# A two-layer hybrid decoder trunk: products without use in the first stage, an interruptible output projection, and one small transfer moved in its queue

## The chip, the cores and the metric

The kernel runs on one NeuronCore of one Trainium2 chip. The metric is the device time of one execution in microseconds, the median of several runs. The core has five engines with a queue each. PE (TensorE) multiplies matrices; PEld is its loading of the stationary operand, which overlaps the products. DVE (VectorE), ACT (ScalarE) and POOL (GpSimd) work element by element. SP (SyncE) issues the transfers here. Each engine takes its instructions strictly in the order in which the program lists them; they wait for each other through semaphores.

## The reference

Two layers over 512 positions (T) of width 1024 (D), float32. Cut to what matters:

```
for l in range(2):
    h = rms_norm(x, norm_pre_mix[l])
    proj = h @ w_in[l]                    # attention q,k,v | delta q,k,v | gate | beta, decay
    mix = concat(dilated_attention(...), gated_delta_rule(...)) @ w_out[l]
    x = x + rms_norm(mix, norm_post_mix[l])
    h = rms_norm(x, norm_pre_ffn[l])
    u = causal_dwconv(h @ ffn_w_in[l], width 3) + bias
    f = (gelu(gate half of u) * up half of u) @ ffn_w_out[l]
    x = x + rms_norm(f, norm_post_ffn[l])
```

The beta and decay columns are 8 of the input projection's columns; everything in the delta rule hangs on them. `rms_norm` needs the sum of squares of a whole row of 1024, so no normed position can go on before both halves of its row are there.

## The kernel before, in words

**Tiling.** The 512 positions are four tiles of 128 positions, t = 0 to 3; x[t] is 128 positions by 1024. A projection wants the position on the free axis, so a normed tile xs is turned on PE (four 128x128 transposes into one PSUM bank for each half s of the row, s = 0, 1) and then split into a rounded part `hh` (ACT copies it out of PSUM as fp32r) and the rest `hl` (DVE subtracts). Weights are treated alike: the staged `st` gives `wh` (ACT) and `wl` (DVE or POOL). Each product is then three: rounded by rounded, and rounded by rest twice (`three`).

**Two projection helpers.** `chan_proj` gives channels by positions, a block of 128 channels at a time; its first four blocks (`early`) are done first for positions 0 to 255 alone (matmuls with 256 columns), so that they can begin when tiles 0 and 1 are turned; between them the turns of tiles 2 and 3 are issued (`turns`). `tok_proj` gives positions by channels, 128 by 512, with four PSUM banks, one for each t. The weights come in `npc` pieces of two 128-row parts; a call of `piece(pc, t)` is six matmuls of 512 columns. The last `tail` pieces are done tile by tile, and after the last of tile t comes `evac(t, ...)`.

**Output projection.** `out_proj` calls `tok_proj` twice, for columns 0 to 511 (`first`) and 512 to 1023 (`second`). All four pieces of the second half are tail pieces, so PE does tile 0 (four pieces, 24 matmuls), then tile 1, 2 and 3. `second` for a tile squares and sums on ACT (`junk<-pm`), takes the root on POOL (`pr`), adds into x[t] on DVE, and calls `after(t)`, which is `pre_norm`: sum of squares of x[t] on ACT (`junk<-x`), root on POOL (`nr`), the normed xs on DVE. `pre_norm` returns `turn`, the function that issues the eight transposes, hh and hl of that tile. The list `turns` holds these functions. Before the change `out_proj` pops one turn after tile 2 is finished and one after tile 3; the other two go to the up-projection's `chan_proj` (`w_f1`, the profile's `in_w_f`), whose first product needs tiles 0 and 1 turned.

**First stage** (layer 0 only). x[0] comes in two transfers and x[1] in one; then the weight `row` of the norm is spread over the partitions by two products of a row of ones (`pn`), copied to `nw`, and tiles 0 and 1 are normed, turned and split. `ident` is the identity matrix of the transposes. The first projection is `chan_proj` over four key blocks (`w_dn`, `late_low`: block 0 does its three kinds of product in three passes). Beside it runs `decay`, which loads the small weights `stb` (32 KB) of the 8 beta and decay columns, splits them (`wba`) and multiplies them with all four tiles.

**Order of the work.** A scheduler writes every engine's list ahead of time from priorities (`prio(pe, other)`, lower goes first, the first number for PE, the second for all others) and from its own estimate of when things are ready. The transfer queue of SP is ordered by the second number: 2.2 for x[2] and x[3], 2.5 for the tables, L + 3 (3 in layer 0, 103 in layer 1) for the decay part. A wait at the head of a list holds up all that stands behind it.

Of the kernel before, what the change touches and what calls it, by code (L numbers as in the profile page):

```python
# [9 lines left out]
F32 = mybir.dt.float32  # L10
# [24 lines left out]
class Engines:  # L35
# [8 lines left out]
    @contextmanager  # L44
    def prio(self, pe, other=None):
        saved = self.levels
        self.levels = (pe, pe if other is None else other)
        yield
        self.levels = saved
# [41 lines left out]
def run(gen):  # L91
    for _ in gen:
        pass
# [3 lines left out]
def hybrid_trunk(ctx: ExitStack, tc: tile.TileContext, a, out):  # L97
# [67 lines left out]
    def residual(t, src, parts=1):  # L165
        v = quad("x")
        n = D // parts
        for s in range(parts):
            nc.sync.dma_start(v.rearrange("p s n -> p (s n)")[:, s * n:s * n + n], src[:, s * n:s * n + n])
        return v  # L170
# [76 lines left out]
    def act_h(k, t):  # L247
        return hh[:, k, t * P:(t + 1) * P], hl[:, k, t * P:(t + 1) * P]

    def tok_proj(load, npc, get_l, tail, evac):  # L250


        ps = [pm.tile([P, T], F32, name="pm") for _ in range(NT)]
        w = {}

        def piece(pc, t):
            for kk in range(2):
                k = pc * 2 + kk
                wh, wl = w[pc][kk * len(w[pc]) // 2]
                k_ = kk % wh.shape[1]  # L260
                three(ps[t], *get_l(k, t), wh[:, k_, :], wl[:, k_, :], k == 0, k == npc * 2 - 1)

        for pc in range(npc - tail):
            w[pc] = load(pc)
            for t in range(NT):
                piece(pc, t)
            yield
        for pc in range(npc - tail, npc):
            w[pc] = load(pc)
        for t in range(NT):  # L270
            for pc in range(npc - tail, npc):
                piece(pc, t)
            evac(t, ps[t])
            yield

    def out_proj(load, npc, get_l, pnw, after, l0, l1, ln, keep_tile):

        keep, turns = {}, []

        def first(t, ps):  # L280
            with prio(ln):
                ss = sp.tile([P, 2], F32, name="pss", bufs=4)
                o = keep_tile(t)
                nc.scalar.activation(o, ps, AF.Copy)
                square_sum(o, ss[:, 0:1])
                nc.vector.tensor_tensor(o, o, pnw[0], op=OP.mult)
                keep[t] = (o, ss)

        def second(t, ps):
            with prio(ln):  # L290
                o, ss = keep[t]
                square_sum(ps, ss[:, 1:2], tag="junk2")
                r = rstd(ss, "p")
                tmp = ev("ptmp")
                nc.vector.tensor_tensor(tmp, ps, pnw[1], op=OP.mult)
                for s, src in ((1, tmp), (0, o)):
                    nc.vector.scalar_tensor_tensor(x[t][:, s, :], src, r, x[t][:, s, :], op0=OP.mult, op1=OP.add)
                turns.append(after(t))

        with prio(*l0):  # L300
            run(tok_proj(lambda pc: load(0, pc), npc, get_l, 2, first))
        with prio(*l1):
            steps = tok_proj(lambda pc: load(1, pc), npc, get_l, 4, second)
            for i, _ in enumerate(steps):
                if i - (npc - 4) >= 2 and turns[0]:
                    turns.pop(0)()
        return turns if turns[0] else []

    def chan_proj(w_src, nblk, early, evac, turns=(), eng=lambda b: None, late_low=False):

# [44 lines left out]
    for l in range(NL):  # L355
# [2 lines left out]

        if l == 0:
            with prio(0):  # L360
                x[0] = residual(0, a["x"][0, 0:P, :], 2)
                row = pair("row", (1, D))
                nc.sync.dma_start(row, a["norm_pre_mix"][0:1, :])
                x[1] = residual(1, a["x"][0, P:2 * P, :])
                nc.sync.dma_start(ident, a["ident"])
                pn, nw = [], []
                for s in range(2):
                    pn.append(ps4("pn", (P, T)))
                    nc.tensor.matmul(pn[s], ones[0:1, :], row[:, s * T:(s + 1) * T], start=True, stop=True)
            with prio(2.2):  # L370
                for t in range(2, NT):
                    x[t] = residual(t, a["x"][0, t * P:(t + 1) * P, :])
            with prio(4, 0):
                turns = [pre_norm(0, pn, 2)]
                turns[0]()
                for s in range(2):
                    nw.append(am("nw"))
                    nc.scalar.activation(nw[s], pn[s], AF.Copy)
                pre_norm(1, nw)()
            with prio(4, 2.1):  # L380
                turns = [pre_norm(t, nw) for t in range(2, NT)]

# [23 lines left out]

        def decay():
            stb = wp.tile([P, KC, 8], F32, name="stb", bufs=1)
            nc.sync.dma_start(stb, a["w_ba"][l])
            wba = wp.tile([P, KC, 16], F32R, name="wba", bufs=1)  # L410
            split(wba[:, :, 0:8], wba[:, :, 8:16], stb)
            pba = ps4(shape=(P, T))
            for k in range(KC):
                nc.tensor.matmul(pba[:16], wba[:, k, :], hh[:, k, :], start=k == 0, stop=False)
                nc.tensor.matmul(pba[:16], wba[:, k, :], hl[:, k, :], start=False, stop=k == KC - 1)
            bas = big("bas")
            nc.scalar.activation(bas[:16], pba[:16], AF.Copy)
            pb2 = ps4(shape=(P, NT, 8))
            for t in range(NT):
                nc.tensor.matmul(pb2[:, t, :], bas[:16, t * P:(t + 1) * P], fold, start=True, stop=True)  # L420
            xa, xb = s16("xa"), s16("xb")
            nc.scalar.activation(v3(xb), pb2[:, :, 0:4], AF.Exp, scale=-1.0)
            nc.vector.tensor_tensor(v3(xa), pb2[:, :, 4:8], dtb[:, None, l * H:(l + 1) * H].to_broadcast([P, NT, H]),
                                    op=OP.add)
            nc.vector.tensor_scalar(xb, xb, 1.0, None, op0=OP.add)
            nc.vector.reciprocal(bet, xb)
            yield
            na, e2, u, d1, cz, rd, lnu, sf = (s16(n) for n in ("na", "e2", "u", "d1", "cz", "rd", "lnu", "sf"))
            nc.vector.scalar_tensor_tensor(na, xa, -1.0, xa, op0=OP.mult, op1=OP.min)
            nc.scalar.activation(e2, na, AF.Exp)  # L430
            nc.vector.tensor_scalar(u, e2, 1.0, None, op0=OP.add)
            nc.scalar.activation(lnu, u, AF.Ln)
            nc.vector.tensor_scalar(d1, u, -1.0, None, op0=OP.add)
            nc.vector.tensor_scalar(cz, d1, 0.0, None, op0=OP.is_equal)
            nc.vector.tensor_tensor(d1, d1, cz, op=OP.add)
            nc.vector.reciprocal(rd, d1)
            nc.vector.tensor_tensor(sf, lnu, rd, op=OP.mult)
            nc.vector.tensor_tensor(sf, sf, cz, op=OP.add)
            nc.vector.tensor_tensor(sf, sf, e2, op=OP.mult)
            nc.vector.scalar_tensor_tensor(sf, xa, 0.0, sf, op0=OP.max, op1=OP.add)  # L440
            ea = sp.tile([P, H], F32, name="ea", bufs=1)
            nc.scalar.activation(ea, alog[:, l * H:(l + 1) * H], AF.Exp)
            nc.vector.scalar_tensor_tensor(v3(gr), v3(sf), -1.0, ea[:, None, :].to_broadcast([P, NT, H]),
                                           op0=OP.mult, op1=OP.mult)
            pg = ps4(shape=(P, 32))
            nc.tensor.matmul(pg[:, :16], tri, gr, start=True, stop=True)
            nc.tensor.matmul(pg[:, 16:], ones, gr, start=True, stop=True)
            nc.vector.tensor_scalar(ng, pg[:, :16], -1.0, None, op0=OP.mult)
            nc.scalar.activation(eg, pg[:, :16], AF.Exp)
            nc.vector.tensor_scalar(neg, eg, -1.0, None, op0=OP.mult)  # L450
            nc.scalar.activation(egl, pg[:, 16:], AF.Exp)

            pgt = ps4(shape=(P, P))
            nc.tensor.matmul(pgt[:16], gr, tri, start=True, stop=True)
            gt = sp.tile([16, P], F32, name="gt", bufs=1)
            nc.vector.tensor_copy(gt, pgt[:16])
            nc.sync.dma_start(dG, gt)
            for t in range(NT):
                Gs.append(big("G", shape=(P, H, P)))
                nc.sync.dma_start(Gs[t].rearrange("p h i -> p (h i)"), bcast(dG, H * P, t * H * P))  # L460
            nc.vector.tensor_tensor(bd, pg[:, 16:], ng, op=OP.add)
            nc.scalar.activation(bd, bd, AF.Exp)
            yield
# [656 lines left out]
```

## Time and profile before

| what | value |
| --- | --- |
| median of 3 runs | 1332.97 us (1331.96 to 1333.19) |
| the profiled execution's own time | 1331.07 us |
| its span | 1329.3 us |
| PE busy in the span | 1297.5 us (98%), 6892 matmuls |
| PE waiting before the first product | 4.2 us |
| PE waiting for ACT's hh, whole span | 4.9 us, 4 times, longest 2.2 us |
| PE waiting for DVE's xs, whole span | 4.9 us, 7 times, longest 1.1 us |
| PE waiting for DVE's wba | 0.7 us, once |

The profiled execution took 1.9 us less than the median of the runs, and its span is 1.8 us shorter than its own time. In the profile's rows a start in us from the span's start is followed by a duration, the engine, the source line (here always that of a helper, L54), the operation, out<-in by the names of the program, the shape, and how many instructions were merged (x8). In brackets stands the idle time of the engine ahead of the row and what ended it. The window rows give, for a stretch, its length, then busy time and number of instructions of PE, PEld, DVE, ACT and POOL, then the granted clock of TensorE (PEclk), the busy share of the DMA engines, and GB/s. Ends of matmuls are modelled, so the distance from start to start tells more than a duration.

### The profile page before, as it was taken

The page shows a single profiled execution, that of the slowest core. Times are in us where ns is not written, and L with a number is a line of the kernel's source. Part 1 is how long each engine was busy: PE and PEld are TensorE (multiplying, and loading weights), DVE is VectorE, ACT ScalarE, POOL GpSimd, SP SyncE. Part 2 cuts the span into 40 slices and gives each one's busy share as a digit, 9 for nine tenths or more (in the row PEclk, how much of TensorE's full clock was granted, in tenths as well). Part 3 has the DMA queues.
Part 4 walks back from the last instruction along what each step waited for, and adds up shares of the span by engine and source line. Part 5 has one row for each costly group of instructions (what it writes and reads, how often), then busy time and mean ns, then how long its engine had stood idle before and what let it go on. Part 6 is the DMA issues. An engine that isn't in the chain of part 4 may idle for free.

```text
span 1329.3 us, 19287 instructions
## 1 busy us (share of the span) xinstructions
PE 1297.5 (98%) x6892; PEld 1082.3 (81%) x6892; DVE 1005.4 (76%) x1938; ACT 728.0 (55%) x1466; POOL 179.4 (13%) x222
## 2 busy tenths in 40 slices
PE   8999999998999999999999999999999999999997
PEld 7787888878888888888778877888888888888876
DVE  6766888967676788798778568989667677888885
ACT  5635976754433344467547369676543334444673
POOL 0019400201000000030011292002010000001201
PEclk9999999999999999999999999999999999999999
DMA  7233211344466566366652422104436565653664
GB/s 241 84 103 96 72 53 37 111 143 135 139 229 212 174 222 218 106 187 180 215 170 77 122 81 76 52 17 135 134 113 208 188 221 203 226 173 116 194 189 159
DMA packets 75425, 193.14 MB, mean 145 GB/s; under 512 B 13345, under 2 KB 13889, under 8 KB 75330
## 3 DMA queue, kind: packets, MB, share of 16 engines
q1 hardware_dynamic: 74882, 190.87, 44.9%
q0 software_dynamic: 448, 1.05, 0.3%
q8 instruction: 54, 0.88, 0.3%
q14 instruction: 41, 0.34, 0.1%
HBM read 161.99 MB, written 29.90 MB: 144 GB/s over the span
## 4 chain that ended last, share of the span: by engine, by line
PE 72%; DVE 6%; ACT 3%; issue 2%; POOL 2%; DMA 1%; POOLq 0%; DVEq 0%; ACTq 0%; SPq 0%
PE pm L54 62%; PE pw L54 10%; DVE wl L54 2%; ACT junk L54 1%; DVE xs L54 1%; DVE x L54 1%; POOL nr L54 1%; DMA st<-in_w_f 1%; ACT wh L54 1%; DVE xf L54 1%; POOL pr L54 1%; DVE hl L54 0%; POOL qs L54 0%; ACT sc L54 0%; DMA G<-dG 0%
## 5 line engine op out<-in xcount | busy, mean ns | idle before, releaser
L54 DVE TENSOR_TENSOR wl<-st,wh 128x1024 fp32r<-128x1024 f32 (+1 forms) x250 | 281.9, 1133 | 167.1 <-ACT wh L54 166.0
L54 ACT ACTIVATE wh<-st 128x1024 fp32r<-128x1024 f32 (+1 forms) x254 | 245.6, 971 | 245.5 <-PE pm L54 225.3
L54 PE MATMUL pm<-hh,wh 128*128 128x512 f32 (+1 forms) x1024 | 372.2, 366 | 4.9 <-ACT hh L54 4.9
L54 PE MATMUL pm<-hh,wl 128*128 128x512 f32 (+1 forms) x1024 | 373.7, 366 | 1.1 <-DVE wl L54 1.1
L54 PE MATMUL pm<-hl,wh 128*128 128x512 f32 (+1 forms) x1024 | 373.5, 366 | 0.0
L54 PEld LDWEIGHTS pm<-hh,wh 128*128 128x128 f32 x1024 | 194.1, 191 | 35.8 <-ACT hh L54 6.2
L54 PEld LDWEIGHTS pm<-hh,wl 128*128 128x128 f32 x1024 | 194.7, 191 | 30.7 <-DVE wl L54 1.3
L54 PEld LDWEIGHTS pm<-hl,wh 128*128 128x128 f32 x1024 | 194.8, 191 | 28.9
L54 PE MATMUL pm<-wh,xf 128*128 128x512 f32 x528 | 164.5, 390 | 0.0
L54 PE MATMUL pm<-wh,hh 128*128 128x512 f32 x384 | 153.3, 401 | 0.0
L54 PE MATMUL pm<-wl,hh 128*128 128x512 f32 x384 | 152.3, 398 | 0.0
L54 PE MATMUL pm<-wh,hl 128*128 128x512 f32 x384 | 151.2, 396 | 0.0
L54 DVE SCALAR_TENSOR_TENSOR fgu<-pm,fw,fgu 128x511 f32<-128x511 f32 (+1 forms) x176 | 131.2, 746 | 21.9 <-ACT fgu L54 19.9
L54 PEld LDWEIGHTS pm<-wh,xf 128*128 128x128 f32 x528 | 99.1, 188 | 21.3 <-ACT e L54 0.6
L54 PE MATMUL pm<-wl,xf 128*128 128x512 f32 x264 | 103.5, 392 | 0.5 <-DVE wl L54 0.5
L54 POOL TENSOR_TENSOR g<-g 128x256 f32<-128x256 f32 x22 | 25.3, 1168 | 493.2 <-DVE xf L54 493.2
L54 PEld LDWEIGHTS pm<-wh,hh 128*128 128x128 f32 x384 | 71.9, 188 | 14.9 <-DVE zs L54 0.6
L54 PEld LDWEIGHTS pm<-wh,hl 128*128 128x128 f32 x384 | 72.4, 189 | 14.0
L54 PEld LDWEIGHTS pm<-wl,hh 128*128 128x128 f32 x384 | 72.4, 189 | 13.6 <-DVE wl L54 0.8
L54 ACT ACTIVATE fgu<-fgu 128x512 f32<-128x512 f32 x44 | 27.8, 632 | 90.4 <-DVE fgu L54 90.4
L54 ACT ACTIVATE fgu<-pm,fb,fw 128x512 f32<-128x512 f32 x88 | 66.9, 760 | 18.6 <-PE pm L54 18.6
L54 ACT ACTIVATE xf<-g 128x256 fp32r<-128x256 f32 x154 | 60.2, 410 | 29.2 <-PE pm L54 22.5
(228 smaller groups left out, 1796.3 us busy)
## 6 DMA issues: line engine op xcount, KB each, us to landing
st<-in_w_f SPq DMA_DIRECT2D x118, 512.0 KB, 3.7
ws<-in_w_f SPq DMA_DIRECT2D x88, 256.0 KB, 4.7
T<-ws SPq DMA_DIRECT2D x66, 256.0 KB, 2.3
st<-in_w_at SPq DMA_DIRECT2D x32, 512.0 KB, 4.0
st<-T SPq DMA_DIRECT2D x30, 512.0 KB, 4.0
st<-in_w_dn SPq DMA_DIRECT2D x24, 512.0 KB, 4.0
st<-in_w_out SPq DMA_DIRECT2D x16, 512.0 KB, 3.7
U<-ws SPq DMA_DIRECT2D x22, 256.0 KB, 2.2
```

What stands on the lines that cost most here:

```text
L54: r = f(*args, **kwargs)
```

## The change

Three things are changed.

**First stage.** PE gets seven products without use, 128 by 128 by 128 in f32, into a PSUM bank of their own (`pwarm`, one of the four `pm` banks): four of `ones` with itself at the very start, one with x[0] behind the two `pn` products, two with nw[0]. The transfer of `row` goes ahead of x[0]. x[1] comes in two transfers, and its squares are summed in two halves.

**Output projection.** `tok_proj` gets an optional function that is called after each tail piece. `out_proj` uses it to pop the turn of tile 0 after the third of the four pieces of tile 2, and that of tile 1 after the third piece of tile 3.

**Small weights.** The transfer `stb` gets its own priority (L + 2.3 in SP's queue): behind x[2] and x[3], ahead of the tables.

```
-    def tok_proj(load, npc, get_l, tail, evac):
+    def tok_proj(load, npc, get_l, tail, evac, between=None):
...
             for pc in range(npc - tail, npc):
                 piece(pc, t)
+                if between:
+                    between(t, pc - npc + tail)
             evac(t, ps[t])
...
         with prio(*l1):
-            steps = tok_proj(lambda pc: load(1, pc), npc, get_l, 4, second)
-            for i, _ in enumerate(steps):
-                if i - (npc - 4) >= 2 and turns[0]:
+            def between(t, i):
+                if (t, i) in ((2,2),(3,2)):
                     turns.pop(0)()
-        return turns if turns[0] else []
+
+            run(tok_proj(lambda pc: load(1, pc), npc, get_l, 4, second, between))
+        return turns
...
             with prio(0):
-                x[0] = residual(0, a["x"][0, 0:P, :], 2)
+                pwarm = pm.tile([P, T], F32, name="pm")
+                def warm(n, moving):
+                    for _ in range(n):
+                        nc.tensor.matmul(pwarm[:, :P], ones, moving[:, :P], start=True, stop=True)
+                warm(4, ones)
                 row = pair("row", (1, D))
                 nc.sync.dma_start(row, a["norm_pre_mix"][0:1, :])
-                x[1] = residual(1, a["x"][0, P:2 * P, :])
+                x[0] = residual(0, a["x"][0, 0:P, :], 2)
+                x[1] = residual(1, a["x"][0, P:2 * P, :], 2)
...
+                warm(1, x[0][:, 0, :])
...
+                warm(2, nw[0])
-                pre_norm(1, nw)()
+                pre_norm(1, nw, 2)()
...
         def decay():
             stb = wp.tile([P, KC, 8], F32, name="stb", bufs=1)
-            nc.sync.dma_start(stb, a["w_ba"][l])
+            with prio(L + 1, L + 2.3):
+                nc.sync.dma_start(stb, a["w_ba"][l])
```

The scheduler then writes other lists at three stretches: the first stage with what follows from it in layer 0, and the end of the output projection in each of the two layers. The down-projection and everything else keep their order.

**Place 1: the start of PE's list.** Before (pn is the spread norm weight, pw a bank of transposes, wh_218 and wh_222 the two halves of key block 0):

```order
L54 MATMUL pn<-row,ones 128x512 x2
L54 MATMUL pw<-ident,xs 128x128 x12
L54 MATMUL pm<-hh,wh_218 128x256 x4
L54 MATMUL pw<-ident,xs 128x128 x4
L54 MATMUL pm<-hh,wh_222 128x256 x4
```

Now (wh_229 and wh_233 are block 0, wh_278 is block 1):

```order
L54 MATMUL pm<-ones 128x128 x4
L54 MATMUL pn<-row,ones 128x512 x2
L54 MATMUL pm<-x,ones 128x128
L54 MATMUL pw<-ident,xs 128x128 x4
L54 MATMUL pm<-nw,ones 128x128
L54 MATMUL pw<-ident,xs 128x128 x4
L54 MATMUL pm<-nw,ones 128x128
L54 MATMUL pw<-ident,xs 128x128 x4
L54 MATMUL pm<-hh,wh_229 128x256 x4
L54 MATMUL pw<-ident,xs 128x128 x4
L54 MATMUL pm<-hh,wh_278 128x256
L54 MATMUL pm<-hl,wh_278 128x256
```

The products without use stand ahead of `pn`, behind it, and between the transposes of tiles 0 and 1. The 16 products of `wba`, which stood some 90 matmuls behind the transposes of tile 3, now follow them directly.

**Place 2: PE's list at the end of the output projection, layer 0.** Before (the wh_33xx are the output projection's weights, wh_3550, wh_3599 and wh_3648 blocks 0 to 2 of the up-projection):

```order
L54 MATMUL pm<-wh_3328,hh 128x512
L54 MATMUL pm<-wl_3329,hh 128x512
L54 MATMUL pm<-wh_3328,hl 128x512
L54 MATMUL pw<-ident,xs 128x128 x8
L54 MATMUL pm<-hh,wh_3550 128x256
L54 MATMUL pm<-hh,wh_3599 128x256
L54 MATMUL pm<-hh,wh_3648 128x256
L54 MATMUL pw<-ident,xs 128x128 x4
L54 MATMUL pm<-hl,wh_3550 128x256
```

Now:

```order
L54 MATMUL pw<-ident,xs 128x128 x8
L54 MATMUL pm<-wh_3335,hh 128x512
L54 MATMUL pm<-wl_3336,hh 128x512
L54 MATMUL pm<-wh_3335,hl 128x512
L54 MATMUL pm<-wh_3339,hh 128x512
L54 MATMUL pm<-wl_3340,hh 128x512
L54 MATMUL pm<-wh_3339,hl 128x512
L54 MATMUL pm<-hh,wh_3561 128x256
L54 MATMUL pm<-hh,wh_3610 128x256
L54 MATMUL pm<-hh,wh_3659 128x256
```

The eight transposes of tile 1 now have six matmuls of tile 3 behind them (those of tile 0 likewise six of tile 2). The first four transposes of tile 2, which stood ahead of `hl,wh_3550`, now stand 23 matmuls later together with the other four.

**Place 3: ACT's list at the same place.** Before (`junk<-x` is the sum of squares of the new x[t], `junk<-pm` that of the second half of the projection's tile, hh the rounded copy of a turned half tile; the first two rows are for tiles 2 and 3, the hh row is tile 1):

```order
L54 ACTIVATE junk,ss<-x 128x1024
L54 ACTIVATE junk,pss<-pm 128x512
L54 ACTIVATE hh<-pw 128x4x128 x2
L54 ACTIVATE wh_3687<-st 128x512
L54 ACTIVATE hh<-pw 128x4x128
L54 ACTIVATE wh<-st 128x1024 x2
L54 ACTIVATE hh<-pw 128x4x128
```

Now (the first hh row is tile 1, the second tile 2):

```order
L54 ACTIVATE hh<-pw 128x4x128 x2
L54 ACTIVATE junk,ss<-x 128x1024
L54 ACTIVATE junk,pss<-pm 128x512
L54 ACTIVATE wh_3698<-st 128x512
L54 ACTIVATE wh<-st 128x1024 x2
L54 ACTIVATE hh<-pw 128x4x128 x2
```

The two hh of tile 1 no longer stand behind the two sums. On DVE the two hl of tile 1, which stood behind the root `nv`, a weight split and the first half of xs of tile 2, now stand ahead of these three; the second half of xs of tile 1 stands behind the two hl of tile 0 instead of ahead of them.

## The prediction

> **What bounds the kernel now.** I read the page first, then PE's waits, then PE's timeline at its longest waits, with the windows' clock beside it.
>
> ```profile
> span 1329.3 us, 19287 instructions
> PE 1297.5 (98%) x6892; PEld 1082.3 (81%) x6892; DVE 1005.4 (76%) x1938; ACT 728.0 (55%) x1466; POOL 179.4 (13%) x222
> PE pm L54 <- ACT hh L54: 4.9, 4, 2.2
> PE pw L54 <- DVE xs L54: 4.9, 7, 1.1
> PE pn L54 <- DMA row<-in_norm_pre_mix: 4.2, 1, 4.2
> ```
>
> PE is the bound: it is busy 98% of the span, and no other engine over 76%. So a microsecond that PE doesn't wait, or doesn't work at half rate, is one off the end, if nothing later waits instead. The change cannot shorten PE's useful work; it can only touch waits and the clock. PE's waits for hh and xs sit where it hands over between stages. The first stage:
>
> ```profile
> 4.23 3.75 PE L54 MATMUL pn<-row,ones 1*128 1x512 f32 x4 [4.23 <-DMA row<-in_norm_pre_mix]
> 7.91 2.98 PE L54 MATMUL pw<-ident,xs 128*128 128x128 f32 x12
> 11.58 1.22 PE L54 MATMUL pm<-hh,wh 128*128 128x256 f32 x4 [0.69 <-ACT hh L54]
> 14.34 1.22 PE L54 MATMUL pm<-hh,wh 128*128 128x256 f32 x4 [0.69 <-ACT hh L54]
> 17.06 1.74 PE L54 MATMUL pm<-hl,wh 128*128 128x256 f32 x8
> 18.64 0.28 PE L54 MATMUL pm<-hh,wh 128*128 128x256 f32 x1
> 18.76 0.28 PE L54 MATMUL pm<-hl,wh 128*128 128x256 f32 x1
> 36.51 0.40 PE L54 MATMUL pw<-hh,wba 128*16 128x512 f32 x1 [0.74 <-DVE wba L54]
> ```
>
> Look at the spacing: eight matmuls of 256 columns take 1.74 us at 17.06, 0.217 each; from 18.64 on the same shape comes every 0.12. PE runs at half rate until about 18.5. The hand-over in the output projection, layer 0:
>
> ```profile
> 304.37 1.03 PE L54 MATMUL pw<-ident,xs 128*128 128x128 f32 x8
> 310.70 1.04 PE L54 MATMUL pw<-ident,xs 128*128 128x128 f32 x8
> 313.93 0.62 PE L54 MATMUL pm<-hh,wh 128*128 128x256 f32 x3 [2.19 <-ACT hh L54]
> 315.32 1.00 PE L54 MATMUL pw<-ident,xs 128*128 128x128 f32 x4 [0.76 <-DVE xs L54]
> 315.97 0.56 PE L54 MATMUL pm<-hl,wh 128*128 128x256 f32 x1
> 325.16 0.63 PE L54 MATMUL pw<-ident,xs 128*128 128x128 f32 x4 [0.54 <-DVE xs L54]
> 315.40:318.80 3.40, 3.40 (x17) 3.40 (x18) 3.34 (x7) 2.45 (x3) 0.55 (x1) 0.50 0.34 136
> 319.00:321.00 2.00, 2.00 (x20) 2.00 (x19) 0.78 (x2) 0.30 (x1) 0.00 (x0) 1.00 0.00 0
> ```
>
> PE has finished the projection and the turn of tile 1 by about 311.7, then stands still until 313.93 and again until 315.32. Right behind that the granted clock is 0.50 for 3.4 us: 17 matmuls where 20 come in 2.0 us at full clock. So the standstill is paid twice: 2.19 + 0.76 + 0.54 = 3.49 us of waits, and half of 3.4, 1.7 us, of slow work. In layer 1 the same:
>
> ```profile
> 969.47 0.62 PE L54 MATMUL pm<-hh,wh 128*128 128x256 f32 x3 [1.35 <-ACT hh L54]
> 970.86 1.09 PE L54 MATMUL pw<-ident,xs 128*128 128x128 f32 x4 [0.76 <-DVE xs L54]
> 980.66 0.63 PE L54 MATMUL pw<-ident,xs 128*128 128x128 f32 x4 [0.55 <-DVE xs L54]
> 970.00:975.00 5.00, 4.24 (x24) 4.18 (x24) 4.93 (x9) 2.91 (x4) 0.55 (x1) 0.66 0.43 156
> ```
>
> 1.35 + 0.76 + 0.55 = 2.66 us of waits; 0.34 of 5 us of clock lost is 1.7 us again.
>
> **The output projection's edit.** Who holds hh up? ACT and DVE, layer 0:
>
> ```profile
> 308.98 1.58 ACT L54 ACTIVATE wh<-st 128x1024 fp32r<-128x1024 f32 x2 [0.95 <-DMA st<-in_w_f]
> 311.67 1.06 ACT L54 ACTIVATE junk<-x 128x1024 bf16<-128x1024 f32 x1 [1.11 <-DVE x L54]
> 313.30 1.07 ACT L54 ACTIVATE hh<-pw 128x512 fp32r<-128x512 f32 x2
> 306.81 1.42 DVE L54 SCALAR_TENSOR_TENSOR xs<-x,nr,norm_pre_ffn 128x512 f32<-128x512 f32 x2 [0.67 <-POOL nr L54]
> 308.14 1.28 DVE L54 TENSOR_TENSOR hl<-pw,hh 128x512 fp32r<-128x512 f32 x2
> 311.49 1.82 DVE L54 TENSOR_TENSOR wl<-st,wh 128x512 fp32r<-128x512 f32 x2
> 315.09 1.28 DVE L54 TENSOR_TENSOR hl<-pw,hh 128x512 fp32r<-128x512 f32 x2
> ```
>
> ACT is free from 310.56, but the turn of tile 1 ends at 311.5, and by its list two sums come first, one of which waits for x. Now the turn stands six matmuls earlier: from 304.37 to 310.70 lie one turn (0.8) and 24 matmuls, so 0.23 each, 1.4 for six. Tile 0's turn starts at 304.37 - 1.4 = 303.0, tile 1's at 309.3. hh of tile 1 then runs at 310.56, behind wh, to 311.6. DVE, in its new order: xs first half to 307.5, hl of tile 0 to 308.8, xs second half to 309.5 (0.2 later than its place on PE; the first four transposes cover it), then the chain of tile 2 as before but 0.25 later, the wl pair to 313.4, hl of tile 1 at 313.4 instead of 315.09, its first half done at 314.1. PE: last six matmuls end at 311.5, the three `hh,wh` at 311.9, then a wait until 314.1 for hl, some 2.0 us. No transposes interrupt there now; those of tile 2 come 23 matmuls later, 2.8 us, at about 316.9, when their xs (two of 0.7 behind hl) is just done. What is late next is tile 3, the wait at 325.16. Its sum on ACT stands behind the second hh of tile 2, whose transposes now come with the first four, some 2 us earlier; so its xs is there at about 323.2. PE at full clock is there at about 322, so it waits about 1.0 where it waited 0.54. Waits left: 3.0 against 3.49, gain 0.5; and the half rate of 1.7 goes, if a standstill of 2.0 doesn't cost the clock. Layer 1: its first wait was 0.84 shorter than layer 0's, so it is about 1.2 now, and the last 1.0: 2.2 against 2.66, gain 0.46, and 1.7. I take 2.2 + 2.2 = **4.4 us**. If the clock still falls, PE reaches tile 3 too late to wait, and only 3.49 - 2.0 and 2.66 - 1.2, 3.0 together, is gained. Upper bound, the tile 3 wait hidden too: 6.4. From there to 660 PE's only wait is this one, so it keeps what it has:
>
> ```profile
> 620.35 0.50 PE L54 MATMUL pm<-wl,xf 128*128 128x512 f32 x1 [0.26 <-DVE wl L54]
> ```
>
> **The first stage's edit.**
>
> ```profile
> 0.75 0.86 SPq L54 DMA_DIRECT2D x<-in_x  x2
> 1.66 0.33 SPq L54 DMA_DIRECT2D row<-in_norm_pre_mix  x1
> 3.38 0.63 ACT L54 ACTIVATE junk<-x 128x512 bf16<-128x512 f32 x1 [1.36 <-DMA x<-in_x]
> 6.86 1.06 ACT L54 ACTIVATE junk<-x 128x1024 bf16<-128x1024 f32 x1 [2.00 <-DMA x<-in_x]
> 16.69 0.75 DVE L54 SCALAR_TENSOR_TENSOR xs<-x,nr,nw 128x512 f32<-128x512 f32 x1 [0.52 <-POOL nr L54]
> 8.00:10.00 2.00, 2.00 (x9) 1.67 (x10) 1.89 (x4) 1.95 (x5) 0.55 (x1) 1.00 1.02 420
> ```
>
> Cost of the products: a `pn` product of 512 columns is two instructions of about 0.85 (four from 4.23 to 7.9 with the drain), so one of 128 columns is a quarter, 0.43, and seven are 3.0 us. Four (1.7) lie in the 4.23 us in which PE waits for `row`; one lies behind `pn`, where PE waits for ident and xs; two (0.9) stand between transposes, ahead of the 0.69 wait for hh that covers most of them. Cost 0 to 0.5. `row` leaves 0.9 earlier and x[0] 0.35 later; x[0] then is the later one, gain 0 to 0.4. The extra transfer of x[1] takes SP about 0.4, hidden because the DMA engines are full (share 1.02, 420 GB/s) and the bytes stay in the same order. Data side: -0.3 to +0.4, taken as +0.2.
>
> The clock is the larger part. 24 matmuls of 256 columns and four transposes between 11.58 and 18.64 run at half rate: 24 x 0.097 + 0.45 = 2.8 us, if PE were the bound there. It isn't throughout: at full rate PE comes to tile 2's transposes at about 16.2 (14.34, less 1.0 for faster transposes and matmuls ahead of it, and 24 matmuls at 0.12), while their xs, paced by ACT and DVE, started at 16.69 and moves little. Bounds 0 and 2.8; I take 1.3, nearer the middle since half is lost to that wait.
>
> The Trainium skill (TensorE: Matmul & The Clock Gate, Part 1: The HAM clock gate) says that the array starts at half clock and is released after a free-running window of about 3.4 us of sustained work, and halved after an idle one; the 3.4 us of 0.50 above agree in length. By that rule PE, occupied by the products and `pn` from the start, would be released before the first transposes, and with the upper bound of 2.8 the time would be 1325.1.
>
> **stb's transfer.** The wait of 0.74 at 36.51 goes, since the split of `stb` now comes ten microseconds earlier; the 16 products now stand right behind tile 3's turn and may wait there for its hl instead. Between 0 and 0.74: 0.5. Tables pushed behind `st` (dmask, tri) are used after 36 us only.
>
> **Sum.** 4.4 + 0.2 + 1.3 + 0.5 = 6.4 us; span 1322.9. The profiled execution took 1331.07, 1.8 over its span and 1.9 under the median of the runs; I take the difference off that median: 1332.97 - 6.4 = **1326.6 us**.
>
> **Rivals.**
>
> *The clock falls again in the hand-over.* For it: 2.0 of 3.4 us still idle in layer 0. Against it: at least 1.4 us of work in any such stretch, where before under 1 us was left. Sum 3.0 + 2.0 = 5.0: 1328.0.
>
> *The early release doesn't happen, or is lost before block 0.* For it: `pn` kept PE occupied from 4.23 to 7.9 and twelve transposes to 10.9, yet the rate rose only at 18.5, after 4 us of dense matmuls. So the filler may count for little and transposes not at all. Sum without the 1.3: 5.1, so 1327.9. The Trainium skill states a rule for this (TensorE: Matmul & The Clock Gate, Part 4: PE-mode transpose): transposes don't count as busy work for the clock; the row at 7.91 agrees with it.
>
> *The turns move but hl doesn't.* hl of tile 1 stays behind tile 2's chain because ACT's hh is late (the split at 308.98 waits for its transfer) and lands where it was. Then only the first stage's 2.0 remains: 1331.0, no change. For it: that wait is a DMA's. Against: ACT has a whole microsecond free before 311.67.
>
> *Slower: PE blocks on a turn that isn't ready.* Once a turn stands inside a tile's matmuls, PE can't go round it. Tile 0's xs is ready 0.4 before its new place, tile 1's 0.2 after it. Were DVE late by D there, PE would stop for about D twice in each layer, 4D; it eats the gain from D = 1.6, and at 2.4 the time is 1332.97 - 6.4 + 9.6 = 1336.2. Against: DVE's chain there is the unchanged one, and D that large is not seen in either layer.
>
> **How the numbers follow.** Forecast 0.46, clock falls again 0.18, no early release 0.18, hl not earlier 0.11, slower 0.05, other 0.02. 0.2% is 2.7 us, about what a measurement of this kernel tells from no change; faster means under 1330.3, which holds for the first three: 0.82. Same 0.12, slower 0.06. Range: best bounds 6.4 + 0.4 + 2.8 + 0.7 = 10.3 down to 1322.7, unlikely together; the worst of the faster cases, both clock rivals at once, 1329.3, and most of the third: 1323.2 to 1330.8.
>
> **What would show it.** PE's spacing of 256-column matmuls at 0.12 before 14 us; the wait of 0.74 gone; the transposes of tiles 0 and 1 about 1.4 us earlier relative to the projection; one wait of 1 to 2 us on hl in the hand-over, no 0.50 in the windows behind it; a wait of about 1 us for tile 3's xs. Half clock behind the hand-over, or a wait on xs inside the output projection, would prove me wrong.

## The result, and the profile after

| | median | range, runs |
| --- | --- | --- |
| before | 1332.91 us | 1331.96 to 1333.19, 4 |
| changed | 1324.86 us | 1321.87 to 1326.42, 4 |

The ratio is 0.9934, with a 95% interval of 0.992 to 0.9948: 8.0 us by the medians, 8.8 by the ratio. The profiled execution of the changed kernel took 1325.45 us.

The head of the page of the changed kernel, and PE's part of its waits (total, times, longest):

```profile
span 1323.7 us, 19323 instructions
PE 1295.8 (98%) x6906; PEld 1080.4 (82%) x6906; DVE 1006.7 (76%) x1938; ACT 729.1 (55%) x1468; POOL 178.8 (14%) x222
```

```profile
PE pm L54 <- DVE hl L54: 2.2, 2, 1.1
PE pm L54 <- ACT hh L54: 1.0, 2, 0.7
PE pw L54 <- DVE xs L54: 5.0, 7, 1.6
```

PE's busy time is 1.7 us less with 14 more instructions: work was not removed, less of it ran at half rate. The wait for hh fell from 4.9 to 1.0, and a wait for hl of 2.2 in two places is new. PE's timeline of the changed kernel at the hand-over of the output projection, layer 0 and then layer 1, and below it the windows there:

```profile
309.26 1.03 PE L54 MATMUL pw<-ident,xs 128*128 128x128 f32 x8
313.08 0.39 PE L54 MATMUL pm<-hl,wh 128*128 128x256 f32 x1 [1.05 <-DVE hl L54]
322.67 0.63 PE L54 MATMUL pw<-ident,xs 128*128 128x128 f32 x4 [0.92 <-DVE xs L54]
966.47 0.39 PE L54 MATMUL pm<-hl,wh 128*128 128x256 f32 x1 [1.15 <-DVE hl L54]
976.01 0.63 PE L54 MATMUL pw<-ident,xs 128*128 128x128 f32 x4 [0.86 <-DVE xs L54]
```

```profile
313.00:315.00 2.00, 1.92 (x16) 1.93 (x17) 1.56 (x5) 0.12 (x1) 0.93 (x1) 1.00 0.75 277
315.00:317.00 2.00, 2.00 (x20) 2.00 (x19) 1.94 (x5) 1.12 (x2) 0.55 (x1) 1.00 0.48 188
968.00:970.00 2.00, 2.00 (x20) 2.00 (x19) 1.89 (x4) 1.06 (x1) 0.40 (x2) 1.00 0.60 244
```

Two waits remain in each layer, 1.97 and 2.01 us together where there were 3.49 and 2.66, and the clock stays at 1.00: 20 matmuls in 2.0 us where 17 had taken 3.4. Counted in matmuls, PE gains 3.2 us on the kernel before across layer 0's hand-over and 2.3 across layer 1's. The timeline of the changed kernel's first stage, PE's rows and the one of ACT that comes into them late:

```profile
1.06 2.07 PE L54 MATMUL pm<-ones 128*128 128x128 f32 x8 [1.06 <-DVE pexp L54]
3.07 3.78 PE L54 MATMUL pn<-row,ones 1*128 1x512 f32 x4
8.04 1.09 PE L54 MATMUL pw<-ident,xs 128*128 128x128 f32 x4 [0.46 <-DMA ident<-in_ident]
12.61 0.74 PE L54 MATMUL pm<-hh,wh 128*128 128x256 f32 x4 [0.69 <-ACT hh L54]
16.02 1.12 PE L54 MATMUL pm<-hl,wh 128*128 128x256 f32 x8
29.93 0.40 PE L54 MATMUL pw<-hh,wba 128*16 128x512 f32 x1 [0.71 <-ACT hh L54]
31.31 0.40 PE L54 MATMUL pw<-hl,wba 128*16 128x512 f32 x1 [0.50 <-DVE hl L54]
28.34 1.06 ACT L54 ACTIVATE wh<-st 128x1024 fp32r<-128x1024 f32 x1 [2.46 <-DMA st<-in_w_at]
```

Full rate is there by 12.6 us (eight matmuls in 1.12 us at 16.02, against 1.74 at 17.06 before), some six microseconds earlier, although the first hh matmul starts 1.0 us later than it did. Counted in matmuls, without those of no use, PE leads by 1.5 us at 16 and at 23 us, and by 0.3 at 45: the wait for `wba` at 36.51 is gone, but its products, now right behind tile 3's turn, wait 0.71 and 0.50 there, because ACT took a weight tile that landed late ahead of tile 3's hh.

### The profile page after: what moved, and what is told of

Read it like the earlier page. It is cut to its first block, busy times and chain, and to the rows that moved or that the text cites. A ratio compares the mean times of both kernels' runs of the same rounds, so it can differ in the third digit from the quotient of the medians.

```text
span 1323.7 us, 19323 instructions
## 1 busy us (share of the span) xinstructions
PE 1295.8 (98%) x6906; PEld 1080.4 (82%) x6906; DVE 1006.7 (76%) x1938; ACT 729.1 (55%) x1468; POOL 178.8 (14%) x222
## 3 DMA queue, kind: packets, MB, share of 16 engines
q0 software_dynamic: 448, 1.05, 0.4%
## 4 chain that ended last, share of the span: by engine, by line
PE 81%; DVE 7%; ACT 5%; DMA 3%; issue 2%; POOL 2%; SPq 1%; POOLq 0%; DVEq 0%; ACTq 0%
PE pm L54 69%; PE pw L54 12%; DVE wl L54 2%; ACT junk L54 1%; ACT wh L54 1%; DVE xs L54 1%; DVE x L54 1%; DMA st<-in_w_f 1%; POOL nr L54 1%; ACT sc L54 1%; DMA x<-in_x 1%; POOL pr L54 1%; SPq L54 1%; DVE xf L54 1%; ACT Vt L54 1%
```

## The experiments

Three groups of four kernels, each group on one chip beside the kernel before (medians 1332.70, 1332.87 and 1332.35 us). Medians are given with the ratio to before and its interval.

**Each part alone.** Only `tok_proj`'s and `out_proj`'s edits are kept:

```
-            steps = tok_proj(lambda pc: load(1, pc), npc, get_l, 4, second)
-            for i, _ in enumerate(steps):
-                if i - (npc - 4) >= 2 and turns[0]:
+            def between(t, i):
+                if (t, i) in ((2,2),(3,2)):
                     turns.pop(0)()
```

> The kernel before with the output projection's edit alone. Theory A (read from the two traces: PE is 0.1 us ahead at 300 us, 3.3 us ahead behind the hand-over of layer 0, 2.6 us more behind that of layer 1): the hand-over is all of the gain, about 5.5 us below the kernel before, 1327.4. Rival B (the prediction's sum): the hand-over is worth 4.4 us, 1328.5, and the rest comes from the first stage. In the profile both expect no half clock behind either hand-over and one wait of about 1 us for hl.

1327.16 us, 0.9963 [0.9953, 0.9973]: 5.5 us by the medians, 4.9 by the ratio. The interval, 3.6 to 6.3 us, holds both expectations. Of its timeline the hand-over in layer 0, and PE's and ACT's rows at the small weights in the first stage; then the window behind the hand-over:

```profile
313.97 0.39 PE L54 MATMUL pm<-hl,wh 128*128 128x256 f32 x1 [1.75 <-DVE hl L54]
36.44 0.40 PE L54 MATMUL pw<-hh,wba 128*16 128x512 f32 x1 [2.46 <-DVE wba L54]
35.78 0.26 ACT L54 ACTIVATE wba<-stb 128x64 fp32r<-128x64 f32 x1 [4.55 <-DMA stb<-in_w_ba]
```

```profile
315.00:317.00 2.00, 2.00 (x11) 2.00 (x10) 1.56 (x4) 1.06 (x1) 0.58 (x1) 0.50 0.77 277
```

In layer 0 the wait for hl is 1.75 us and the clock does fall; in layer 1 it is 0.85 and the clock holds. The rows at 36 us show something else: in this execution the clock happened to be released at 11.1 us, PE came 1.8 us ahead to the wait for `wba`, and waited 2.46 there instead of 0.74. `stb` lands when it lands; a lead won ahead of it is given back.

The first stage alone is the diff's products, `row` first, and x[1] in two, with the other two edits left out:

> The kernel before with the first stage's edit alone (seven products without use, row first, x[1] in two); small weights where they were. Theory A: the clock is released early and PE is about 1.5 us ahead at 23 us; with the 16 wba products at their old place nothing takes that back, so 1.0 to 1.5 us under the kernel before, 1331.5. Rival B: 1.5 us, the same. Rival C (the first stage is worth nothing because x[1] and ident land later): no difference, 1332.9.

1329.77 us, 0.9981 [0.9972, 0.9991]: 2.9 us by the medians, more than any of the three expectations; the interval, 1.2 to 3.7 us, excludes only the third, that it is worth nothing. PE's lead in its profile is 2.5 us at 45 us. It loses 1.7 of them near 171 us, where PE works through 32x32 matmuls behind a wait for Z, a tile of the delta rule. Its timeline there and at the hand-over of layer 0, and the window behind Z:

```profile
168.59 0.22 PE L54 MATMUL pw<-Z,UT 32*32 32x32 f32 x2 [0.84 <-DVE Z L54]
312.20 0.62 PE L54 MATMUL pm<-hh,wh 128*128 128x256 f32 x3 [1.21 <-ACT hh L54]
```

```profile
171.00:174.00 3.00, 3.00 (x12) 2.80 (x12) 2.95 (x8) 2.05 (x5) 0.00 (x0) 0.50 0.07 29
```

The clock fell to 0.50 for one window. And the hand-over in layer 0 is unedited, yet its wait for hh is 1.21 us and not 2.19; that row is taken up further down. The clock fell behind this hand-over all the same, from 313.93 us for 3.41.

Small weights alone, and everything but small weights:

```
-            nc.sync.dma_start(stb, a["w_ba"][l])
+            with prio(L + 1, L + 2.3):
+                nc.sync.dma_start(stb, a["w_ba"][l])
```

> The kernel before with the small weights' transfer moved alone. Theory A: the 16 wba products now stand behind tile 3's transposes and wait there for hh and hl (0.71 and 0.50 us in the trace after) behind a weight split that waits for its transfer; this costs more than the 0.74 us that it saves: 0.3 to 1 us slower, 1333.5. Rival B (the prediction): 0.5 us faster, 1332.4.

> The changed kernel with the small weights' transfer put back. Theory A: about 1 us faster than the changed kernel, because the first stage's 1.5 us are kept: 1323.8, 9 us under the kernel before. Rival B: 0.5 us slower than the changed kernel, 1325.4.

1332.70 us, 1.0002 [0.9993, 1.001] alone; 1324.83 us, 0.9944 [0.9931, 0.9956] without it. The move is worth nothing that the runs can tell (by the interval between 0.9 us faster and 1.3 slower): the intervals of both runs hold the theory's time and the rival's. The single parts add up: 5.5 + 2.9 + 0 = 8.4 us, against 8.0 for all.

**What in the first stage does it.** The changed kernel without its seven products, twice, the second time beside the changed kernel itself; and the changed kernel with neither products nor the small weights' move:

```
-                warm(4, ones)
-                warm(1, x[0][:, 0, :])
-                warm(2, nw[0])
```

> The changed kernel without its seven products without use; row first, x[1] in two, the turns and the small weights' place all stay. Theory (the products are what sets PE's clock free early, at 11.72 in the changed kernel, and with it comes the 2.5 to 2.9 us that the first stage was worth by itself): the clock is released later, by one window of 3.4 us or two, the lead of 1.7 us at 16 us is not there, and the time is 1327.0 to 1327.8. Rival (it is the transposes or the other two edits of the stage; with the output projection alone the clock was released at 11.14 without any product): release between 10 and 14 us again, time 1324.4 to 1325.6.

> The changed kernel without its seven products, a second time, now beside the changed kernel on the same chip. Theory (the products are worth about 2 us, as the first measurement had it against the first of the changed kernel): 1.5 to 2.5 us over the changed kernel of this group. Rival (the clock is released at 10 to 11 us by the transposes alone, and the products hold up PE's first hh matmul by 1.2 us, 12.61 against 11.42): within 0.8 us of it, to either side.

> The changed kernel without its seven products and with the small weights' transfer in its old place: what is left is row first, x[1] in two, and the interruptible output projection. Theory (neither of the two left out is worth anything that can be measured): within 1 us of the changed kernel of this group. Rival (products worth 2 us): 1.5 to 2.5 us over it.

> The changed kernel once more, as the yardstick beside the three others of this group, and for a second profile of its first 45 us: in its first one PE's lead on the kernel before was 1.7 us at 16 us and 0.3 at 45, though the stage was worth 2.5 to 2.9 by the runs. Theory (what was lost there, a wait of 2.46 us of ACT for a weight tile at 28.34 among it, is the transfers' chance from one execution to the next): lead of 1 to 2.5 us at 45 us in this profile, time 1324.2 to 1325.6. Rival (the loss belongs to the change): the same wait of ACT, lead under 0.5 again, time the same.

| | median, us | ratio to before |
| --- | --- | --- |
| without products | 1326.78 | 0.9954 [0.9941, 0.9967] |
| without products, again | 1325.48 | 0.9948 [0.9935, 0.9962] |
| without products and small weights' move | 1327.79 | 0.9961 [0.9946, 0.9976] |
| the change again | 1324.24 | 0.9940 [0.9926, 0.9954] |

In the first run without products the clock was released at 10.3 us, as the rival had it, and the time fell between the two ranges named. Within the one group the products are worth 1.2 us, with intervals that overlap: between the two expectations. Over all runs (9 of the change, the result's four and this group's five, with a mean of 1324.5 us; 10 without products, from two groups, with 1326.1) they are worth 1.6 us, with 1.2 to either side; not all of these ran beside each other. The clock's release is not what tells these two kernels apart: by the trace's clock records it came at 11.7 and 17.5 us with products, at 10.3 (and lost again for 3.4 us) and 17.8 without. Over all fourteen profiles it did come early more often with products: by 12.6 us in five of seven, against two of seven without. The kernel that lacks the small weights' move too lies further off than either theory had it; its profile lost the clock near 173 and 316 us. The second profile of the change has no late weight tile in the first stage and a lead of 0.8 us at 45 us, below the 1 to 2.5 expected.

What does tell them apart lies 290 us later. Ahead of the sums of layer 0's hand-over ACT splits a tile of `in_w_f`. First its row and that of PE's wait for hl in the change's second profile, and from the DMA view of 4 us around the issue of three such tiles the median time from issue to landing (ACT's split waits for the first of the three, which took 3.8 us here and 4.6 in the kernel shown next):

```profile
293.69 0.63 ACT L54 ACTIVATE wh<-st 128x512 fp32r<-128x512 f32 x1 [2.18 <-DMA st<-in_w_f]
312.11 0.39 PE L54 MATMUL pm<-hl,wh 128*128 128x256 f32 x1 [1.18 <-DVE hl L54]
```

```profile
st<-in_w_f SPq DMA_DIRECT2D x3, 512.0 KB, 4.2
```

The same of the second run without products; here the DMA view has one packet of the queue of instruction code as well (packets, MB, share):

```profile
295.14 0.63 ACT L54 ACTIVATE wh<-st 128x512 fp32r<-128x512 f32 x1 [3.03 <-DMA st<-in_w_f]
313.57 0.39 PE L54 MATMUL pm<-hl,wh 128*128 128x256 f32 x1 [2.02 <-DVE hl L54]
```

```profile
q8 instruction: 1, 0.02, 1.4%
st<-in_w_f SPq DMA_DIRECT2D x3, 512.0 KB, 4.8
```

And of the kernel before, ACT's row and the DMA view:

```profile
295.53 0.63 ACT L54 ACTIVATE wh<-st 128x512 fp32r<-128x512 f32 x1 [2.84 <-DMA st<-in_w_f]
```

```profile
q8 instruction: 1, 0.02, 1.5%
st<-in_w_f SPq DMA_DIRECT2D x3, 512.0 KB, 4.9
```

A 16 KB piece of instruction code is fetched in the middle of the w_f tiles in the second and third kernel. In the first the trace has the same fetch 8.6 us ahead of ACT's split, before these tiles are issued. PE's list is 14 matmuls longer there, each with its weight load, and the other engines' lists are the same as without products, so the likely reading is that PE crosses a boundary of its code earlier.

All fourteen profiles of this study fall in two groups by this. In the seven with products the fetch comes 8.6 to 12.2 us ahead of the split, and ACT waits 1.8 to 2.2 us for the tile; in the seven without, it comes 2.2 to 3.4 us ahead of it, and ACT waits 2.8 to 3.5. The distance grows with what was put into PE's list ahead of this place: 8.6 to 9.1 us in the five profiles with 14 matmuls more, 10.7 in the one with 20 and 12.2 in the one with 26 (both further down). The first of the three tiles takes 3.4 to 3.8 us from issue to landing in the seven, and 4.6 to 4.8 in the three of the others whose trace has its landing; the two behind it do not differ so (5.1 and 5.0 us with products in everything but small weights). Of these fourteen, the ten with the edited projection then wait for hl 0.8 to 1.2 us (six with products) or 1.75 to 2.02 (four without).

The clock fell behind that wait in none of the six, and in three of the four. In the profiles the products' gain is here: PE wins 3.1 to 3.5 us across layer 0's hand-over with them, 1.6 to 2.1 without (the edited kernels). The other runs bear out the clock's part of it only weakly: the mean granted clock is 0.9974 over the 9 runs of the change, 0.9973 over the 10 without products, and 0.9962 over the 6 that lack the small weights' move too; a single fall of 3.41 us takes 0.0013. The shorter wait for hl is 0.6 to 1.2 us; how much of the rest of the 1.6 us is clock stays open. That the fetch delays the tile is argued from the fourteen profiles; no run moved the fetch by itself.

**Rows of products and the clock.** `pn` made over 128 rows, and seven products at the start:

```
-                warm(4, ones)
-                row = pair("row", (1, D))
-                nc.sync.dma_start(row, a["norm_pre_mix"][0:1, :])
+                warm(7, ones)
+                row = pair("row", (P, D))
+                nc.gpsimd.memset(row, 0.0)
+                nc.sync.dma_start(row[0:1, :], a["norm_pre_mix"][0:1, :])
...
-                    nc.tensor.matmul(pn[s], ones[0:1, :], row[:, s * T:(s + 1) * T], start=True, stop=True)
+                    nc.tensor.matmul(pn[s], ones, row[:, s * T:(s + 1) * T], start=True, stop=True)
```

> The changed kernel, but pn is made by products over 128 rows instead of one (the row tile is zero below its first row, POOL clears it, row's transfer leaves behind x[0]), and seven products stand at the start instead of four (ten in all). Theory (one-row products don't count for the clock, whole ones do): a window of 3.4 us full of whole products lies between 1.1 and 7.9 us, and matmuls stand at full spacing somewhere from 4.5 to 7.9, not at 11.7; pn costs half of its 3.78 then; PE waits for x and ident anyway, so the time moves little, 1323.9 to 1324.9. Rival (rows don't matter, the clock goes by a window that began too late): release at 10 to 12 us as before, time 1324.9 to 1325.6 as row comes later.

1327.52 us, 0.9963 [0.9948, 0.9978]. The first theory was right on the clock and wrong on the time. PE and one row of ACT:

```profile
4.64 1.94 PE L54 MATMUL pn<-row,ones 128*128 128x512 f32 x4
7.92 0.66 PE L54 MATMUL pw<-ident,xs 128*128 128x128 f32 x4 [1.34 <-DVE xs L54]
10.64 0.49 PE L54 MATMUL pm<-nw,ones 128*128 128x128 f32 x2 [2.06 <-ACT nw L54]
13.77 1.06 PE L54 MATMUL pw<-ident,xs 128*128 128x128 f32 x4
9.47 0.63 ACT L54 ACTIVATE wh<-st 128x512 fp32r<-128x512 f32 x1 [2.52 <-DMA st<-in_w_dn]
```

`pn` takes 1.94 us where it took 3.78: the clock was released at 4.76, the earliest of all. But PE then waited 1.34 and 2.06 us for data, and by 13.77 four transposes take 1.06 us again instead of 0.66: the clock was lost at 11.6. An early release without work to keep PE busy is given back.

Which windows release it? The window of 3.4 us ahead of the release in this kernel:

```profile
1.35:4.76 3.41, 3.41 (x17) 3.41 (x17) 0.00 (x0) 1.99 (x5) 0.80 (x2) 1.00 0.77 240
```

The same in the first run without products:

```profile
6.85:10.26 3.41, 2.98 (x12) 2.28 (x12) 2.40 (x6) 2.65 (x6) 0.56 (x1) 1.00 1.02 410
```

And three windows that released nothing, counted back from the later release in steps of 3.41 us. Two are of the kernel before, the first mostly `pn`, the second mostly transposes; the third is of the change's second profile, with transposes and products without use:

```profile
4.81:8.23 3.42, 3.42 (x6) 0.99 (x5) 1.10 (x4) 1.42 (x4) 0.55 (x1) 1.00 1.00 389
8.23:11.64 3.41, 2.72 (x13) 1.99 (x11) 3.01 (x5) 3.10 (x7) 0.55 (x1) 1.00 1.03 419
7.29:10.70 3.41, 3.08 (x14) 2.49 (x13) 1.95 (x5) 2.41 (x6) 0.56 (x1) 1.00 0.99 392
```

(These rows print a clock of 1.00 ahead of the first record; the spacing of the matmuls shows half.) Whole products did release it. So did a window that holds nothing but the twelve transposes, with PE busy 2.98 of 3.41 us; in the kernel with the projection's edit alone it rose behind twelve transposes too. With 2.72 us of the same it did not. But PE's busy time does not settle it: the third window has 3.08 us of it and released nothing. A window full of one-row products released nothing, and the clock of that kernel rose ten microseconds later. So transposes seem to count for the clock in these runs, and one-row products seem not to; how full a window has to be, these rows do not say. That is read from windows in different kernels; this experiment alone, with three more products at the start, doesn't prove it. The Trainium skill says the opposite of transposes (TensorE: Matmul & The Clock Gate, Part 4: PE-mode transpose); the measurement decides.

**x[1] in one transfer.**

```
-                x[1] = residual(1, a["x"][0, P:2 * P, :], 2)
+                x[1] = residual(1, a["x"][0, P:2 * P, :])
```

> The changed kernel with x[1] in one transfer and one sum, as it was; PE's list is the same. Theory (the halves are what made x[1] late: ACT's sum began at 7.81 where the whole tile's began at 6.86, ident at 8.04 kept PE 0.46, and PE's first hh matmul was 1.0 us behind the kernel before): ACT's sum at 6.9 to 7.2, no wait for ident, first hh matmul up to 1 us earlier, time 1323.9 to 1324.4. Rival (the DMA engines are full there, share 1.0, and it is the order of row and x[0] that costs): sum at 7.5 or later, time 1324.9 +- 0.4.

1326.02 us, 0.9946 [0.9933, 0.9959]. ACT's and PE's rows:

```profile
7.84 1.06 ACT L54 ACTIVATE junk<-x 128x1024 bf16<-128x1024 f32 x1 [2.35 <-DMA x<-in_x]
13.14 0.74 PE L54 MATMUL pm<-hh,wh 128*128 128x256 f32 x4 [0.69 <-ACT hh L54]
```

The sum begins at 7.84, as late as with halves, and the first hh matmul is later. The halves are not what made x[1] late; the rival holds, with a time somewhat over what it named.

**The clock by itself.** The kernel before, with eight products without use in the gap:

```
+            fill = ps4("fill")
+            for _ in range(8):
+                nc.tensor.matmul(fill[:, 0, :], ones, ones, start=True, stop=True)
         return turns if turns[0] else []
```

> The kernel before, its turns where they were, with eight products of 128 columns without use put into PE's gap behind tile 1's turn at the end of each output projection (some 1.7 us at full clock, 3.4 at half); nothing else is added. Theory (half of what the output projection's edit brings is the half clock of 3.4 us behind the gap, 1.7 us in each layer, and the gap's idle share is what halves the clock): windows behind the gap at clock 1.00, waits on hl and xs as in the kernel before less what the products take up, time 1329.3 to 1331. Rival (the gain was the waits alone and the half clock was hidden by them, since tile 2's and tile 3's xs set the end of that stretch): 1332.3 to 1333.1.

1330.02 us, 0.9978 [0.9967, 0.9988]: 2.9 us (1.6 to 4.4 by the interval) for nothing but useless work. PE's timeline in layer 0, and the window behind:

```profile
311.97 1.95 PE L54 MATMUL fill<-ones 128*128 128x128 f32 x16
314.97 0.39 PE L54 MATMUL pm<-hh,wh 128*128 128x256 f32 x1 [1.05 <-ACT hh L54]
316.86 0.39 PE L54 MATMUL pm<-hl,wh 128*128 128x256 f32 x1 [1.50 <-DVE hl L54]
```

```profile
317.00:319.00 2.00, 2.00 (x17) 2.00 (x18) 1.94 (x5) 1.08 (x2) 0.55 (x1) 1.00 0.41 168
```

PE gets to real work no earlier, but at full clock; counted in matmuls, this one profile gains 0.5 us across layer 0's hand-over and 1.1 across layer 1's. Over all runs the mean granted clock says the same: 0.9975 here, 0.9953 for before in this group; 0.0022 of 1330 us is 2.9, the whole gain. The theory holds. By the same sum 2.4 us of the projection's edit (0.9973 against 0.9955) and 2.7 of the whole change in its second measurement (0.9972 against 0.9952) are clock. This mean counts the last 3 to 5 us of every profile, which ran at half clock, and not the time ahead of the first release. It also shows that the change still loses clock in some executions: its single runs lie between 0.996 and 0.999, both its profiles at 0.998.

**Z's wait filled.** Everything but small weights, with three products ahead of each of the two groups of Z's 32x32 matmuls in each layer:

```
                 pp = ps4(shape=(P, 2, H, NB))
+                for _ in range(3):
+                    nc.tensor.matmul(pp[:, 0, :, :], ones, ones, start=True, stop=True)
```

> The changed kernel with the small weights' transfer back in its old place, and with three products of 128 columns without use ahead of the 32x32 matmuls of Z in each layer, where PE waits 0.7 us for Z near 170 us and near 823 us, and where four of ten profiles show half clock for 3.4 us; the planner moves some instructions around that place. Theory (these windows are what still costs clock, and the products take it away): no half clock near 171 to 177 us, mean granted clock 0.998, time 0.5 to 1.2 us under that kernel without them, 1323.6 to 1324.4. Rival (the products push the chain of Z, or the new order costs as much): 1324.8 to 1326.

1331.68 us, 0.9997 [0.9985, 1.0008]: it gives all of the gain back, more than the rival named. Three rows say why the test is inconclusive:

```profile
166.17 0.83 PE L54 MATMUL pw<-ones 128*128 128x128 f32 x6
169.91 0.41 PE L54 MATMUL pw<-Z,UT 32*32 32x32 f32 x8 [0.93 <-DVE Z L54]
263.72 0.58 PE L54 MATMUL pw<-R,Z 128*128 128x128 f32 x1 [2.31 <-DVE R L54]
```

The scheduler put the products three microseconds ahead of the wait, not into it, and moved the work around it. The clock near 171 us stayed at 1.00 in this profile, but the new order of the layer cost more: in place of two waits of 1.03 and 0.39 us near 260 us in the change's profiles stands one of 2.31, for R, another tile of the delta rule, and clock was lost there instead. The drop near 171 us, seen in five of the fourteen profiles, is left unmended.

No version tried here beats the change by more than the runs can tell; without the small weights' move it is as good.

## Why the prediction was right, and where it was not

The forecast was 1326.6 us, with 1323.2 to 1330.8; 1324.86 was measured. The sum of 6.4 us stands against 8.0.

**Output projection, 4.4.** Alone it brought 5.5 us by the medians (3.6 to 6.3 by the interval of the ratio). Both of its halves are there, but not in the sizes forecast, 1.0 of waits and 3.4 of clock: by the profile of this edit alone the waits fell by 2.6 us (1.75 for 3.49, and 0.85 and 1.00 for 2.66), and by the mean granted clock 2.4 us are clock. That the clock counts by itself is shown by the useless work in the gap, which brought 2.9. In layer 1 each number came as worked out (waits 1.15 and 0.86 for 1.2 and 1.0, 2.3 us gained for 2.2). In layer 0 the wait for hl was forecast at 2.0 and measured at 1.05. The step that failed is DVE's chain taken "as before but 0.25 later": it rested on a weight tile's landing in the trace of before, and the tile lands some 1 us earlier in the profiles where PE's list is longer. Without the products the wait was 1.75 to 2.02, as forecast, and then the forecast's other condition, that a standstill of 2.0 us keeps the clock, fails three times in four. So in the profile of the projection's edit alone the rival "the clock falls again" was right in layer 0; in the two of the whole change it wasn't, and the shorter wait behind that came with the first stage, for a reason no step had in it. That the total came out near the forecast is in part luck: a smaller gain in clock and a larger one in waits made up for each other.

**First stage, 1.5.** Alone 2.9 us (1.2 to 3.7 by the interval). The mechanism named, a release of the clock in time for block 0, is there in the profile: full spacing at 12.6 us. But the release varies from execution to execution, between 10.1 and 17.5 us in the six profiles with these products and `pn` as in the change, and the profile of the change shows hardly any of it left at 45 us. A term that the forecast lacks is the shorter wait at layer 0's hand-over, 1 us in its own profile (1.21 for 2.19), where the code fetch comes early too; the clock fell there as before. The rival "no early release" held in one of the change's two profiles, at 17.5 us, and not in the other, at 11.7.

**Small weights, 0.5.** The wait of 0.74 is gone, and products do wait for tile 3 instead, as the lower bound had it: 1.2 us in one profile of the change, nothing in the other. No gain was measured. That does not contradict 0.5 us, which lies inside the interval of the run.

**The rest.** hl does come earlier, so that rival is out. No wait for xs inside the output projection appeared: the slower rival's price was never asked.

By the Trainium skill (TensorE: Matmul & The Clock Gate, Part 1: The HAM clock gate) the window is about 3.4 us and runs free of the program. The trace's records agree: the single falls last 3.41 us each, and their place in the program shifts with the execution, so that the same kernel can lose 1.7 us at a wait or not.

## What to carry to other kernels

A standstill of two microseconds on the engine that sets the time can cost another 1.7 us in clock behind it, so it is worth splitting a stall in two, or filling it with useless products placed exactly there, even if no data comes earlier. A lead won early is kept only up to the next thing that comes at its own time, such as the landing of a transfer. And where an edit adds instructions to a long list, later effects need not come from what the edit does: compare the landing of transfers, and the fetch of instruction code, before a gain is put down to the clock.

## What was not expected of the hardware

- With fourteen matmuls more on PE at the start a 16 KB code fetch 285 us later came ahead of the weight tiles instead of among them. ACT's wait for the tile was 1.8 to 2.2 us instead of 2.8 to 3.5, without exception in fourteen profiles. That the one causes the other is argued.
- The clock was released behind a window of 3.4 us with twelve transposes alone, PE busy 2.98 us, and behind one of whole products, as early as 4.76 us. It was not behind a window full of one-row products, nor behind one of transposes and useless products with PE busy 3.08 us.
- The clock fell behind a wait of 1.75 to 2.02 us in three of four profiles, and behind one of 0.8 to 1.2 in none of six. In the unedited hand-over of layer 1 it fell in three of the three profiles with neither filler nor edit.
- Matmuls of 32x32 behind a wait of 0.7 to 0.8 us can cost the clock though PE shows as busy: between 170 and 176 us it fell in five of fourteen profiles.
